# A masked-prefix-sum gather on one core: the rest rows move between the block places on TensorE, and the idle matmuls ahead of each wait are 10, 4 or none instead of 3

## The chip, the core and the metric

The kernel runs on one core of one Trainium2 chip. The metric is the device time of one execution in microseconds; lower is better. The kernel before took 84.66 us (median of four runs, 84.47 to 85.42).

## What is computed

```python
B, S, D = x.shape                       # 8, 8192, 512, float32
mask = (pos < lengths[:, None, None])   # rows past a sequence's length are zero
cs = np.cumsum(x * mask, axis=1)
midpoints = (lengths // 2).clip(0)
mid_features = cs[b_idx, midpoints, :]
return np.matmul(mid_features[:, None, :], w).squeeze(1)
```

Only row `lengths // 2` of each cumulative sum is used. So for each of the 8 sequences the kernel adds up its first `n = min(lengths // 2 + 1, lengths)` rows of 512 numbers, and multiplies the 8 sums by `w` (512 x 512). For the lengths of this case `n` is 570, 2690, 256, 2057, 905, 3772, 3859 and 571.

## The kernel before

**Blocks, places and rests.** Each sequence's `n` rows are cut into whole blocks of 512 rows (1 MB each; 128 partitions x 4 rows) and a rest of fewer than 512 rows. The sum over rows is a matmul: the weights are a 128 x 8 matrix that says to which of the 8 sequences a partition's rows belong, the rows are the moving operand, and `s_ps` in PSUM accumulates. A block takes four float32 matmuls (`add`, L490 to L494), which the profile shows as 8 matmul records, a pair of blocks as 16.

- The first block of sequences 0 and 1 is loaded blindly into `first`, before the lengths are known, and the last whole block of sequence 7 into `last`, in three pieces, at the very end.
- The other whole blocks (23 here) go in pairs through three *places* (`NS = 3`) of the buffer `xt`, 2 MB each. One round fills and uses the three places once, so 23 blocks take 4 rounds; the fourth has two full pairs and a single block in the third place.
- The rests go through two buffers of `rem` (`q = 0, 1`), two sequences a round, so 4 rounds as well. A rest is loaded by up to four smaller DMAs.

**Who does what.** SyncE (SP) loads the places: `load(k)` (L207 to L232) waits until place `k` is free, then issues its DMA, and after the rounds the three pieces of `last` (L246). ScalarE's queue loads the rests (L276, L288), each when its buffer is free. TensorE does the matmuls. VectorE (DVE) waits for a place's or a rest's matmuls, writes the next weights (`cur` L456, `cur_rem` L464) and by that frees the place or the rest's buffer. All the waits are on semaphores by hand; `take(eng, s, n)` (L144 to L146) waits for `n` and takes it off again. Each engine runs its own loop over rounds, in the order in which the code stands.

**TensorE's round** (L534 to L554) is: wait for rest 0 and add it, wait for rest 1 and add it; then for each place: three matmuls on constant data whose result nobody reads (`keep_busy`, L502 to L505, tile `idle_ps`, in bfloat16), the wait for the place (`take(pe, s_full[k], 32)`, L544), a branch on whether the place holds one block or two (L545), and the matmuls. `pairs` (L148 to L153) nests the places: a place that has no block any more ends the round.

**After the rounds** a one-element matmul (`tell`, L507 to L510) signals that the sum is complete. DVE copies `s_ps` to `s_sb` in two halves; TensorE transposes and folds it by matmuls (`fold_half`) and adds the pieces of `last` between them (`add_last`, L558), both into `t_ps`; DVE transposes into `t_sb`; TensorE multiplies by `w` into `o_ps`; DVE and ScalarE copy the two halves of the result to `o_sb`, and SP and ScalarE's queue store them.

## Time and profile before

| | |
|---|---|
| time, median of 4 runs | 84.66 us (84.47 to 85.42) |
| time of the profiled execution | 84.47 us |
| its span, first to last instruction | 82.5 us |
| PE busy / DVE busy / ACT busy | 56.1 / 15.2 / 5.5 us |
| matmuls of pairs (L492, `xt`) | 184 records, 25.1 us |
| idle matmuls (L505) | 48 records, 15.4 us |
| matmuls of rests (L492, `rem`) | 64 records, 9.9 us |
| moved by DMA | 31.26 MB |

The span is what the profiler sees of the execution; 1.97 us of the profiled time lie around it. A busy time is a sum over one engine, and the engines run beside each other, so busy times do not add up to the span. All positions below are microseconds from the start of the span. The notation `x16` after a group counts records, and `[3.52 <-PEq L146]` says that the engine sat idle for 3.52 us before it, released by the wait on line 146, which is that of `take`. `PEclk` is the share of TensorE's full clock that was granted.

### The profile page before, as it was taken

Reading aid. Unit: us, or ns where it says so; the run is one execution under the profiler, and the core shown is the slowest. Engines: PE = TensorE matmul, PEld = TensorE weight load, DVE = VectorE, ACT = ScalarE, POOL = GpSimd, SP = SyncE. Lnnn points to the kernel's source line nnn. Section 1 sums busy time; section 2 is a strip of 40 time slices with the busy share of each in tenths; the row PEclk is TensorE's granted clock in tenths of the full one; section 3 lists DMA queues with packets and bytes.
Section 4 is the critical chain, followed back from the end, with each engine's and each line's share of the span. In section 5 each row is a group of like instructions: output and inputs, shape, how many; then the busy total and the mean of one; then the engine's idle time right before and its main releaser. Section 6 shows DMA issues by size and latency. Waiting matters only on the chain. (4 is left out here: it accounts for less than half of the span.)

```text
span 82.5 us, 1486 instructions
## 1 busy us (share of the span) xinstructions
PE 56.1 (68%) x389; PEld 13.2 (16%) x389; DVE 15.2 (18%) x79; ACT 5.5 (7%) x6; POOL 1.6 (2%) x13
## 2 busy tenths in 40 slices
PE   2950699739990298930990799938408999799730
PEld 2300101002110121200110211111101112123510
DVE  2858888100000001000000001000000000001420
ACT  2991000000000000000000000000000000000020
POOL 5100000000000000000000000000000000000000
PEclk9999999999999999999759857999965569999996
DMA  2899999999999998999999999999999999899000
GB/s 36 306 413 437 461 419 415 443 439 397 445 437 405 397 476 361 433 417 437 441 401 436 442 413 421 453 425 397 456 405 446 397 437 453 373 403 366 1 0 16
DMA packets 3539, 31.26 MB, mean 379 GB/s; under 512 B 530, under 2 KB 546, under 8 KB 1202
## 3 DMA queue, kind: packets, MB, share of 16 engines
q1 hardware_dynamic: 2610, 27.27, 78.5%
q10 hardware_dynamic: 928, 3.97, 12.4%
q8 instruction: 1, 0.02, 0.1%
HBM read 31.23 MB, written 0.02 MB: 379 GB/s over the span
## 5 line engine op out<-in xcount | busy, mean ns | idle before, releaser
L492 PE MATMUL s_ps<-xt,cur 128*8 128x512 f32 x184 | 25.1, 666 | 15.3 <-PEq L146 15.3
L505 PE MATMUL idle_ps<-idle 128*128 128x512 bf16 x48 | 15.4, 436 | 3.6 <-DVE since L340 3.6
L492 PE MATMUL s_ps<-rem,cur_rem 128*8 128x512 f32 x64 | 9.9, 736 | 1.9 <-PEq L146 1.9
L456 DVE TENSOR_TENSOR cur<-since 128x16 f32 x9 | 1.7, 186 | 40.9 <-DVEq L146 40.9
L492 PEld LDWEIGHTS s_ps<-xt,cur 128*8 128x8 f32 x184 | 4.1, 91 | 28.9 <-issue 28.9
L505 PEld LDWEIGHTS idle_ps<-idle 128*128 128x128 bf16 x48 | 3.7, 104 | 21.1 <-issue 19.6
L310 ACT COPY o_sb<-o_ps 8x128 f32<-8x128 f32 x2 | 0.5, 258 | 72.6 <-PE o_ps L586 72.5
L261 ACT ACTIVATE rem<-rem 128x2048 uint32<-128x2048 uint32 x2 | 3.7, 1902 | 0.0
L492 PEld LDWEIGHTS s_ps<-rem,cur_rem 128*8 128x8 f32 x64 | 2.2, 113 | 9.6 <-issue 9.6
L516 PE MATMUL s_ps<-zero 1*128 1x512 f32 x2 | 2.1, 1136 | 1.6 <-DVE zero L340 1.6
L492 PE MATMUL s_ps<-first,cur_first 128*8 128x512 f32 x16 | 2.9, 816 | 0.0
L340 DVE COPY s_sb<-s_ps 128x256 f32<-128x256 f32 x2 | 0.8, 424 | 9.6 <-PE idle_ps L509 9.6
L464 DVE COPY cur_rem<-table 128x32 f32 x6 | 1.1, 181 | 8.1 <-DVEq L146 8.1
L498 PE MATMUL t_ps<-last,e_last 128*8 128x128 f32 x32 | 1.7, 273 | 0.0
L261 ACT ACT_TABLE_LOAD x1 | 1.3, 1283 | 1.4 <-PEq L607 1.4
L586 PE MATMUL o_ps<-wt,t_sb 128*8 128x128 f32 x32 | 1.1, 273 | 0.4 <-DVE t_sb L340 0.4
L340 DVE TENSOR_TENSOR part_a<-since,step_a 1x42 f32<-1x42 f32 (+1 forms) x2 | 1.1, 562 | 0.1
L498 PEld LDWEIGHTS t_ps<-last,e_last 128*8 128x8 f32 x32 | 0.9, 89 | 0.4 <-issue 0.3
L586 PEld LDWEIGHTS o_ps<-wt,t_sb 128*8 128x8 f32 x32 | 0.8, 89 | 0.7 <-issue 0.7
L498 PE MATMUL t_ps<-s_sb,fold 128*8 128x128 f32 x8 | 0.8, 274 | 0.1
L340 DVE TENSOR_TENSOR since<-item,begin 1x42 f32<-1x42 int32 (+1 forms) x2 | 0.8, 422 | 0.1
L519 PEld LDWEIGHTS n_ps<-len_f,ones 1*128 1x128 f32 x2 | 0.7, 333 | 1.0 <-DVE len_f L340 0.5
(66 smaller groups left out, 13.3 us busy)
## 6 DMA issues: line engine op xcount, KB each, us to landing
xt<-in_x_dram SPq DMA_DIRECT2D x10, 2048.0 KB, 12.7
xt<-in_x_dram SPq DMA_DIRECT2D x3, 1024.0 KB, 9.8
first<-in_x_dram SPq DMA_DIRECT2D x2, 1024.0 KB, 7.9
rem<-in_x_dram ACTq DMA_DIRECT2D x3, 512.0 KB, 8.6
wt<-in_w_dram ACTq DMA_DIRECT2D x1, 1024.0 KB, 4.8
rem<-in_x_dram ACTq DMA_DIRECT2D x3, 256.0 KB, 7.8
last<-in_x_dram SPq DMA_DIRECT2D x1, 512.0 KB, 6.1
last<-in_x_dram SPq DMA_DIRECT2D x2, 256.0 KB, 6.3
```

What stands on the lines that cost most here:

```text
L261: act.memzero(rem[:, q]).then_inc(s_rfree[q], 1)
L310: copy = act.copy(out=o_sb[1][:, j * P:(j + 1) * P], in_=o_ps[64 + 32 * j:64 + 32 * j + B, :P])
L340: do(*args, **kw).then_inc(s_dve, 1)
L456: dve.tensor_tensor(out=cur[:, k], in0=since[:, :B, here].rearrange("p b h -> p h b"), in1=since[:, 1:, here].rearrange("p b h -> p h b"), ...
L464: dve.tensor_copy(out=cur_rem[:, q], in_=rests[:, ds(dve.snap(of, min_val=1, max_val=B // 2 - 1), 1), q].rearrange("p o w -> p (o w)"),).t ...
L492: return pe.matmul(s_ps[32 * j:32 * j + B], lhsT=weights, rhs=rows, start=False, stop=False, skip_group_check=True, tile_position=(0, 32 * j))
L498: return pe.matmul(t_ps[32 * j:32 * j + B, :P], lhsT=weights, rhs=row[:, P * j:P * (j + 1)], start=False, stop=False, skip_group_check=Tru ...
L505: pe.matmul(idle_ps[:], lhsT=idle[:, :P], rhs=idle[:], start=True, stop=True)
L516: pe.matmul(s_ps[:], lhsT=zero[:], rhs=zero[:, :1].to_broadcast((1, D)), start=True, stop=False, skip_group_check=True)
L519: pe.matmul(n_ps[:, :B], lhsT=ones[:], rhs=len_f[:], start=True, stop=True).then_inc(s_pe, 1)
L586: mm = pe.matmul(o_ps[32 * j:32 * j + B, :P], lhsT=t_sb[:, kc, :B], rhs=wt[:, kc, j * P:(j + 1) * P], start=(kc == 0), stop=(kc == KC - 1) ...
```

## The change

TensorE's round now takes the places and the rests in turn: place 0, rest 0, place 1, rest 1, place 2. VectorE's loop follows in the same order, since it answers TensorE's signals one by one. The idle matmuls change from three ahead of each place to ten ahead of place 0, two ahead of rest 0, four ahead of place 1, and for place 2 four if it holds a pair and none if it holds a single block. Three idle matmuls ahead of the first round are dropped. The wait for a place now stands behind the branch on one block or two (once in each arm) where it stood ahead of it. `pairs` gets a parameter `most`, with which it does one place only; the places are no longer nested. The loads on SP and ScalarE's queue keep their code.

```diff
-    def pairs(eng, n, body, k=0):
-
-        if k < NS:
+    def pairs(eng, n, body, k=0, most=NS):
+
+        if k < most:
             with eng.If_cmp(n, 2 * k + 1, "IS_GE"):
                 body(k)
-                pairs(eng, n, body, k + 1)
+                pairs(eng, n, body, k + 1, most)
...
-            with dve.If_cmp(rest_rounds, 1, "IS_GE"):
-                for q in range(2):
-                    take(dve, s_rdone[q], 1)
-                    dve.tensor_copy(
-                        out=cur_rem[:, q],
...
-                    ).then_inc(s_rfree[q], 1)
-            pairs(dve, left, weights)
+            for k in range(NS):
+                pairs(dve, left, weights, k, k + 1)
+                if k < 2:
+                    with dve.If_cmp(rest_rounds, 1, "IS_GE"):
+                        take(dve, s_rdone[k], 1)
+                        dve.tensor_copy(
+                            out=cur_rem[:, k],
...
+                        ).then_inc(s_rfree[k], 1)
...
-        keep_busy()
+        BUSY = [10, 4, 0]
         pe.wait_ge(s_dve, DVE_MASK)
         with pe.Fori(0, rounds):
-            with pe.If_cmp(rest_rounds, 1, "IS_GE"):
-                for q in range(2):
-                    take(pe, s_rem[q], 16 * (len(PARTS) + 1))
-                    for j in range(G):
-                        mm = add(j, cur_rem[:, q, j * B:(j + 1) * B], rem[:, q, j])
-                    mm.then_inc(s_rdone[q], 1)
-
             def add_pair(k):
-                keep_busy()
-                take(pe, s_full[k], 32)
-                with pe.If_cmp(left, 2 * k + 2, "IS_GE"):
+                def second():
+                    take(pe, s_full[k], 32)
                     for j in range(G):
                         add(j, cur[:, k, 1], xt[:, k, 1, j])
+
+                keep_busy(BUSY[k])
+                with pe.If_cmp(left, 2 * k + 2, "IS_GE"):
+                    if k == NS - 1:
+                        keep_busy(4)
+                    second()
+                with pe.Else():
+                    take(pe, s_full[k], 32)
                 for j in range(G):
                     mm = add(j, cur[:, k, 0], xt[:, k, 0, j])
                 mm.then_inc(s_done[k], 1)
 
-            pairs(pe, left, add_pair)
+            for k in range(NS):
+                pairs(pe, left, add_pair, k, k + 1)
+                if k < 2:
+                    with pe.If_cmp(rest_rounds, 1, "IS_GE"):
+                        if k == 0:
+                            keep_busy(2)
+                        take(pe, s_rem[k], 16 * (len(PARTS) + 1))
+                        for j in range(G):
+                            mm = add(j, cur_rem[:, k, j * B:(j + 1) * B], rem[:, k, j])
+                        mm.then_inc(s_rdone[k], 1)
             less(pe, left, PER)
             less(pe, rest_rounds, 1)
```

## The prediction

> **What bounds the kernel now.** I read the slices of the page first, to see which resource is never idle.

> ```profile
> PE   2950699739990298930990799938408999799730
> PEclk9999999999999999999759857999965569999996
> DMA  2899999999999998999999999999999999899000
> ```

> PE has holes everywhere. The DMA row has none from the second slice to the 37th, where it stops for good. Four stretches (columns: length, busy time and count of each engine, granted clock, DMA share, GB/s) say how full it is:

> ```profile
> 10.00:76.00 66.00, 48.81 (x320) 10.02 (x323) 6.67 (x33) 0.00 (x0) 0.00 (x0) 0.90 1.01 423
> 20.00:22.00 2.00, 2.00 (x19) 0.43 (x11) 0.18 (x1) 0.00 (x0) 0.00 (x0) 1.00 1.04 442
> 22.00:24.00 2.00, 2.00 (x18) 0.34 (x16) 0.00 (x1) 0.00 (x0) 0.00 (x0) 1.00 1.01 426
> 66.00:68.00 2.00, 2.00 (x16) 0.33 (x8) 0.19 (x1) 0.00 (x0) 0.00 (x0) 0.63 0.98 418
> ```

> A share of 1.01 over 66 us: the 16 DMA engines have no gap that a better order on TensorE could fill. It is no lower around 22 and 67, where the longest idle places are being issued again (at 22.59 and 66.98). The chain of waits names PE for 7% of the span and begins only at 71.95, so I read the end one by one, in order of time (start, length, engine).

> ```profile
> 71.95 0.27 issue
> ...
> 72.22 1.90 PE L492 MATMUL s_ps<-xt,cur 128*8 128x512 f32 x16 [0.46 <-PEq L146]
> 74.06 0.82 PE L505 MATMUL idle_ps<-idle 128*128 128x512 bf16 x3
> 74.82 1.04 PE L492 MATMUL s_ps<-xt,cur 128*8 128x512 f32 x8
> 75.68 0.17 PE L509 MATMUL idle_ps<-idle 128*1 128x1 bf16 x1
> ...
> 76.97 0.26 PEld L498 LDWEIGHTS t_ps<-last,e_last 128*8 128x8 f32 x8
> ```

> and, from the answer on the tile `last`,

> ```profile
> L246 SPq DMA_DIRECT2D last<-in_x_dram x3: 332/333/333, 69.5 to 70.6; - x3
> DMA to landing us min/median/max: 6.1/6.2/6.4
> ```

> The third piece of `last` is issued at 70.57 and lands some 6.35 later, at 76.92. Its weights load starts at 76.97. So the end is set twice over: by the landing of the last bytes, and, with almost no slack, by the sum that `tell` reports at 75.68 (the two copies to `s_sb` take 0.88 from 75.97, and the second fold's weights load starts at 76.90).

> **The change part by part, in the last round, where it can count.** Landings are issue plus time to landing: place 2 of round 3 at 61.90 (49.39 + 12.5), round 4's places at 66.98 (54.78 + 12.2), 71.87 (59.07 + 12.8), 74.38 (66.98 + 7.4).
> - *Wait behind the branch.* From 71.95 the chain shows 0.27 of "issue": the branch that follows the wait. Now the branch is decided while the engine waits. Saved: 0 to 0.27; I take 0.22, since the load for `last`, a wait without a branch behind it, started 0.05 after its landing.
> - *Rest 1 between places 1 and 2.* 8 records, as in the single block: 75.68 - 74.82 = 0.86 added behind the last long wait. Before, this work lay ahead of it.
> - *No idle matmuls ahead of the single block.* 74.82 - 74.06 = 0.76 saved (0.25 each).
> - Sum for `tell`: -0.22 + 0.86 - 0.76 = -0.12, so 75.56. The single block landed at 74.38; TensorE reaches it at 71.87 + 0.14 + 1.84 + 0.86 = 74.7, so no new wait.
> - *For the end.* `add_last` of the third piece can't start before 76.92, and started at 76.97. Of the 0.12 at most 0.05 reaches the end. The profiled 84.47 becomes 84.42.

> This holds if TensorE is ready when place 1 lands. Walk from 61.90 at full clock, a pair at 72.22 to 74.06 = 1.84: pair to 63.9; ten idle matmuls, 2.5, to 66.4; place 0 landed 66.98, pair to 68.95; two idle 0.5, rest 0.86, four idle 1.0: 71.3. Slack 0.55 there and 0.6 at place 0. The eleven extra idle matmuls of a round (2.8) are thus paid from waits (3.52 ahead of 62.21 alone); without that cover they would cost all of it.

> *Earlier rounds.* Place 0 is worked on ahead of the rests, so it is free, and its next DMA issued, up to 2 earlier (two rests, 1.9 or more). SP's `last` pieces move ahead with it. The queue already holds 5 or more of transfers at each issue (22.59 against a next landing at 27.96; 66.98 against 71.87), so this shifts nothing at the end: taken at zero; if the queue did run dry now and then, it would be a gain.

> *Rests.* Their buffers are freed up to 3.5 later (rest 1 of round 3 at about 58.7 where the last ScalarE issue was at 56.0). They land within 5.6 to 9.4 of the issue: by 69 for rest 1, wanted at 73.9, and by 64 for rest 0, wanted at 69.4. Behind TensorE's wait for a rest now stand places 1 and 2, and behind those DVE's `cur` updates and SP's loads; with 5 of slack, nothing. DVE's operations (0.18 and 0.19 each) are the same ones in another order.

> *Branches.* A few more per round; they last 0.07 (not taken) to 0.24 and TensorE's queue is filled ahead of them: zero, bounded by 0.24.

> [...]

> **The clock.** I cut the span at the steps of the granted clock (third number from the end):

> ```profile
> 26.50:29.93 3.43, 1.66 (x16) 0.48 (x20) 0.00 (x0) 0.00 (x0) 0.00 (x0) 1.00 0.96 406
> 43.58:47.00 3.42, 1.20 (x12) 0.36 (x16) 0.00 (x0) 0.00 (x0) 0.00 (x0) 1.00 1.02 429
> 47.00:50.40 3.40, 3.40 (x20) 0.77 (x16) 0.32 (x2) 0.00 (x0) 0.00 (x0) 0.50 0.99 421
> 57.24:60.65 3.41, 1.45 (x11) 0.21 (x3) 0.19 (x1) 0.00 (x0) 0.00 (x0) 1.00 1.04 438
> 60.65:64.06 3.41, 1.85 (x12) 0.47 (x16) 0.00 (x0) 0.00 (x0) 0.00 (x0) 0.50 1.02 429
> 64.06:67.48 3.42, 3.42 (x24) 0.66 (x16) 0.19 (x1) 0.00 (x0) 0.00 (x0) 0.50 0.98 417
> ```

> A stretch of 3.41 with 1.45 busy or less is followed by half clock, one with 1.66 is not; from half clock a stretch with 1.85 busy doesn't lead back, a full one does. The change shortens the longest waits from 3.4-3.6 to 2.1-2.9 (place 2 of round 3: ready at 59.7, landed 61.9). Drops get rarer, not impossible. One stretch at half clock from 62.0 costs the pair and five idle matmuls about 1.6, and the slack of 0.6 + 0.55 takes most of it. So clock alone gives nothing to a kernel that waits for DMA.

> [...]

> **Rivals.**
> 1. *Slower: half clock for two stretches in round 4's approach.* Price, with the row of before (half clock 60.65 to 67.48, pair 62.21 to 65.58 = 3.37, idle at the same ratio 0.46 each): place 2's pair to 65.4; 4.5 idle to 67.5; 5.5 idle 1.35, pair 1.84, idle 0.5, rest 0.86, idle 1.0 to 73.0; pair, rest, block 3.56: `tell` at 76.55, 0.87 late and all of it on the end: 85.3, or 85.5 on the median. It decides once `tell` is later than about 75.7. For it: rest 1 and twice as many idle matmuls now stand in the way; against: the stretch after a drop would have to be half idle again, and behind 62.0 nothing is idle. 12%. Other delays of TensorE's last round, a fetch stall among them: 4%.
> 2. *Faster: earlier issues make the stream denser.* A stream 1.3% faster (428 for 423 GB/s over 66) ends 0.85 earlier: 83.8 on the median; at the 442 of the best row shown, 2.8 earlier. For it: single stretches exceed 423; against: the stretches around the latest issues aren't lower. 14%, small gains mostly.
> 3. *It does not change the waits:* clock falls as often, rests wait. Still 84.4 to 84.7, since DMA ends at 76.9.

> **How the numbers follow.** The profiled run lay 0.19 below the median of 84.66; forecast -0.05 to -0.12: 84.55 on the median, 84.2 to 85.0 by the spread of the runs. A measurement of this kernel tells about 1%, 0.85, from no change. Forecast and rival 3 within 1%: 70%. Slower 16%, faster 14%. The range takes in rival 1 and the edge of rival 2: 83.8 to 85.6.

> **What would show it.** After: DMA share still 1.0 to about 76.9; `tell` near 75.6, 16 + 8 + 8 records without an idle matmul ahead of it; the third `last` load right behind its landing. Wrong if DMA ends before 76.2, or if place 1 of round 4 lands while TensorE is still busy ahead of it.

## The result, and the profile after

The change made the kernel slower: 85.96 us (median of 12 runs, 85.39 to 86.61) against 84.64 us (17 runs), a ratio of 1.0147 with a 95% interval of 1.0111 to 1.0184. The forecast was 84.55 us in a range of 83.8 to 85.6. In all that follows the ratios and their intervals leave out a kernel's runs over 1.5% above its fastest; medians and lists of times hold every run.

The profiled execution took 85.49 us with a span of 83.7. Here are two rows of its slices and part of its DMA rows. The kernel before had one packet of the kind `instruction` (behind the stream, at 80.6) and 366 GB/s in the 37th slice:

```profile
DMA  2799999999999999999999999999999999995000
GB/s 35 294 407 423 470 419 454 411 423 407 462 392 423 442 421 370 427 454 431 423 423 442 395 446 399 411 442 423 427 427 431 414 455 395 411 389 211 4 8 8
DMA packets 3540, 31.28 MB, mean 374 GB/s; under 512 B 530, under 2 KB 546, under 8 KB 1202
...
q8 instruction: 2, 0.03, 0.2%
```

The stream is as dense as it was, up to 76. What is new is one packet more, of the kind `instruction`, and a tail behind the stream. The tail is seen best in stretches of half a microsecond (columns as in the prediction; the last two are DMA share and GB/s). Before:

```profile
76.00:76.50 0.50, 0.36 (x16) 0.07 (x11) 0.47 (x2) 0.00 (x0) 0.00 (x0) 1.00 0.46 164
76.50:77.00 0.50, 0.50 (x16) 0.35 (x20) 0.35 (x1) 0.00 (x0) 0.00 (x0) 1.00 0.00 0
```

and after:

```profile
76.00:76.50 0.50, 0.50 (x12) 0.10 (x3) 0.00 (x0) 0.00 (x0) 0.00 (x0) 1.00 0.80 291
76.50:77.00 0.50, 0.45 (x9) 0.01 (x1) 0.00 (x0) 0.00 (x0) 0.00 (x0) 1.00 0.08 29
77.00:77.50 0.50, 0.50 (x16) 0.33 (x16) 0.43 (x2) 0.00 (x0) 0.00 (x0) 1.00 0.06 25
77.50:78.00 0.50, 0.50 (x20) 0.33 (x16) 0.42 (x1) 0.00 (x0) 0.00 (x0) 1.00 0.03 12
```

A share of 0.06 is one sixteenth, and 25 GB/s are about one sixteenth of the 420 or so of the stream: for over a microsecond only as much moves as one of the 16 DMA engines carries, so I read that one engine still works and the other fifteen are done. The completion signals say since when. A load of this kernel signals 16 times, and TensorE's pair follows the last of them: in this profile place 1 of round 4 signals from 71.49 to 73.19, and its pair begins at 73.32. Before, the 16 signals of place 0 in round 4 come from 66.54 to 66.96; after, from 66.25 to 68.21. The first signals are not late, the last one is. In the first round the spread is still 0.5 to 0.8 us; from 32 on it is 1.6 to 2.7 in every load of SP's queue. In between lies the packet. The DMA part of the stretch from 31.3 to 32.5 (packets, MB, share of 16 engines):

```profile
q1 hardware_dynamic: 49, 0.38, 80.7%
q10 hardware_dynamic: 30, 0.03, 8.4%
q8 instruction: 1, 0.02, 5.6%
```

5.6% of 16 engines over 1.2 us are 1.07 us of one engine: 16 KB of instructions, fetched in the middle of the data at 31.34. And this is the end (order of time, TensorE):

```profile
71.90 1.04 PE L506 MATMUL idle_ps<-idle 128*128 128x512 bf16 x4
73.32 1.90 PE L493 MATMUL s_ps<-xt,cur 128*8 128x512 f32 x16 [0.39 <-PEq L146]
75.04 1.05 PE L493 MATMUL s_ps<-rem,cur_rem 128*8 128x512 f32 x8
75.89 1.05 PE L493 MATMUL s_ps<-xt,cur 128*8 128x512 f32 x8
76.75 0.17 PE L510 MATMUL idle_ps<-idle 128*1 128x1 bf16 x1
77.00 0.62 PE L499 MATMUL t_ps<-last,e_last 128*8 128x128 f32 x16
...
78.26 0.41 PE L499 MATMUL t_ps<-last,e_last 128*8 128x128 f32 x8
```

Pair, rest, block and `tell` follow one another as forecast (3.43 us, forecast 3.56 from the first matmul), but the pair begins at 73.32 where it was due at 72.0, because place 1 landed at 73.19 in place of 71.85. From the answer on the tile `last`:

```profile
L246 SPq DMA_DIRECT2D last<-in_x_dram x3: 333/333/333, 70.1 to 71.1; - x3
DMA to landing us min/median/max: 6.9/7.0/7.1
```

The third piece was issued at 71.1, half a microsecond later than before, and took 7.1 in place of 6.4: it landed at 78.21, 1.29 later, and the span is 1.2 longer.

The twelve times fall into two groups of six, 85.39 to 85.64 (granted clock 0.955 to 1.0) and 86.28 to 86.61 (0.928 to 0.939). The profile above is of the first.

### The profile page after: what moved, and what is told of

Same layout as the page of the kernel before. It is cut to its first block, busy times and chain, and to the rows that moved or that the text cites. A ratio compares the mean times of both kernels' runs of the same rounds, so it can differ in the third digit from the quotient of the medians.

```text
span 83.7 us, 1578 instructions
## 1 busy us (share of the span) xinstructions
PE 62.6 (75%) x426; PEld 16.1 (19%) x426; DVE 15.2 (18%) x79; ACT 5.5 (7%) x6; POOL 1.6 (2%) x13
## 5 line engine op out<-in xcount | busy, mean ns | idle before, releaser
L493 PE MATMUL s_ps<-xt,cur 128*8 128x512 f32 x184 | 24.3, 648 | 11.9 <-PEq L146 11.7
L506 PE MATMUL idle_ps<-idle 128*128 128x512 bf16 x85 | 23.8, 412 | 3.6 <-DVE since L340 3.6
L506 PEld LDWEIGHTS idle_ps<-idle 128*128 128x128 bf16 x85 | 7.1, 101 | 27.6 <-issue 22.1
L493 PE MATMUL s_ps<-rem,cur_rem 128*8 128x512 f32 x64 | 8.6, 607 | 0.0
L493 PE MATMUL s_ps<-first,cur_first 128*8 128x512 f32 x16 | 3.5, 975 | 0.0
L493 PEld LDWEIGHTS s_ps<-rem,cur_rem 128*8 128x8 f32 x64 | 1.4, 89 | 4.6 <-issue 4.6
L517 PEld LDWEIGHTS s_ps<-zero 1*128 1x128 f32 x2 | 0.5, 308 | 1.6 <-DVE zero L340 1.6
```

Of the source, the lines that this page charges most:

```text
L493: return pe.matmul(s_ps[32 * j:32 * j + B], lhsT=weights, rhs=rows, start=False, stop=False, skip_group_check=True, tile_position=(0, 32 * j))
L506: pe.matmul(idle_ps[:], lhsT=idle[:, :P], rhs=idle[:], start=True, stop=True)
L517: pe.matmul(s_ps[:], lhsT=zero[:], rhs=zero[:, :1].to_broadcast((1, D)), start=True, stop=False, skip_group_check=True)
```

## The experiments

Three theories are tested. Theory F (fetch): the loss is the instruction packet, which holds one DMA engine back for the rest of the stream; it comes because the longer program passes a certain length, which I took to be 512 instructions, an assumption that no run had shown. Theory S (schedule): it is the new order, whose rests and places are loaded at other times. Theory C (clock), for the second group: half clock in the last round. "Instructions" below are those of TensorE's program as built, 503 before and 537 after; the kernel's own end is 12 ahead of the total, since the program's closing instructions follow it.

**The changed kernel again** (no edit).

> The changed kernel once more, unchanged. Theory F (fetch): its profile shows a 16 KB instruction packet while the data stream runs, which before has only at 80.6 us after it; one of the 16 DMA engines falls behind by about that packet (1.07 us) and stays behind, so the 16 completions of a load are spread over 1.7 us in place of 0.4, and the last piece lands 1.3 us later. Expected: the packet again, 85.4 to 86.6. Of the twelve times six lie at 85.4 to 85.6 (granted clock 0.955 to 1.0) and six at 86.3 to 86.6 (0.93 to 0.94). Theory C (clock): the second 0.9 us is the half clock of rival 1 and a profile that falls there shows the signal of the complete sum about 0.9 us behind the landing chain. Theory S (schedule): the lateness comes from the order of rests and places; the packet is a bystander.

85.90 us (85.45 to 86.76, ratio 1.0142, interval 1.0079 to 1.0206), again three times at 85.5 and three at 86.3 to 86.8. The packet is there at 30.74, and the last piece lands at 78.26. The profile fell into the second group; it is read below, with the clock.

**Code that never runs**, in the kernel before.

```diff
         with pe.Else():
+            keep_busy(17)
             fold_half(0)
             fold_half(1).then_inc(s_pe, 1)
```

> The kernel before, with 17 idle matmuls (34 instructions) put into the arm of the last branch that these lengths never take: nothing more is executed, but TensorE's program has 537 instructions in place of 503, as many as the changed kernel. Theory F: an instruction packet turns up in the stream, the completions of later loads spread to 1.5 to 2 us, the time rises by 0.9 to 1.4 us, to 85.5 to 86.1. Theory S: nothing executed differs, so 84.6 to 84.7.

85.70 us (85.47 to 86.03), ratio 1.0129, interval 1.0088 to 1.0170. The arm is not executed (1486 instructions in the profile, as before), the order is that of before, and the price is there. Its DMA part, and a stretch of its tail:

```profile
q8 instruction: 2, 0.03, 0.2%
```

```profile
77.00:77.50 0.50, 0.50 (x15) 0.25 (x11) 0.00 (x0) 0.00 (x0) 0.00 (x0) 1.00 0.07 29
77.50:78.00 0.50, 0.50 (x21) 0.21 (x8) 0.34 (x1) 0.00 (x0) 0.00 (x0) 1.00 0.06 25
```

The packet came at 32.38; the signals of the last loads spread over 2.0 to 2.1 us; the last piece landed at 78.51. As nothing executed differs from the kernel before, theory S can't explain any of this.

**The changed kernel without the arm that is never taken.** Nothing that it executes differs.

```diff
-        with pe.Else():
-            fold_half(0)
-            fold_half(1).then_inc(s_pe, 1)
```

> The changed kernel with the arm that is never taken left out, and nothing else: every instruction that the changed kernel executes is executed here, in the same order, and TensorE's program is 18 instructions shorter (519; its last own instruction is number 507). Theory F with the boundary at 512: no instruction packet in the stream, spread of completions 0.4 to 0.6 us, and a median 1.0 to 1.3 us under the changed kernel's 85.9, at 84.5 to 85.0 (two groups 0.5 to 0.9 us apart stay, by theory C). If the order, the idle matmuls or the clock explain the whole of it: 85.9.

84.67 us (84.17 to 86.14), ratio 1.0000, interval 0.9963 to 1.0036. 18 instructions fewer, never executed in either, and 1.29 us are gone: the whole loss. The median stands between groups here too: six runs at 84.17 to 84.42, four at 84.93 to 85.08, and two later. Its DMA part has no row for instructions at all, and the end is the one that was forecast:

```profile
q1 hardware_dynamic: 2610, 27.27, 78.5%
q10 hardware_dynamic: 928, 3.97, 12.2%
```

```profile
72.06 1.90 PE L493 MATMUL s_ps<-xt,cur 128*8 128x512 f32 x16 [0.59 <-PEq L146]
73.77 1.05 PE L493 MATMUL s_ps<-rem,cur_rem 128*8 128x512 f32 x8
74.63 1.05 PE L493 MATMUL s_ps<-xt,cur 128*8 128x512 f32 x8
75.49 0.17 PE L510 MATMUL idle_ps<-idle 128*1 128x1 bf16 x1
...
77.03 0.41 PE L499 MATMUL t_ps<-last,e_last 128*8 128x128 f32 x8
```

`tell` at 75.49 (forecast 75.56); the third piece lands at 76.98, and its matmuls start at 77.03.

**Where the boundary is.** The never-executed lines again, 4, 12 and 22 instructions in place of 34 (`keep_busy(2)`, `(6)`, `(11)`).

> The kernel before with 4 instructions (2 idle matmuls) in the arm that is never taken: TensorE's program has 507 instructions. [...] If every added instruction costs, or the code behind the loop being moved at all, 84.6 to 85.7.

> The same with 12 instructions (6 idle matmuls): 515 instructions, just past 512. Theory F: the whole price at once, a packet in the stream, spread of completions 1.5 to 2 us, 85.4 to 86.0, as with 34 instructions. A cost by the amount of code: a third of the 1.2 us, 84.9.

> The kernel before with 22 instructions (11 idle matmuls) in the arm that is never taken: 525 in all, the last own instruction number 513. With 12 it was 515 and 503, and nothing happened. Boundary at 512 for the program's own end: the packet and 85.4 to 86.0. If the boundary lies elsewhere (between 525 and 537 in all): 84.5.

| instructions (own end) | packet in the stream | third piece lands | median us | ratio, interval |
|---|---|---|---|---|
| 503 (491), before | none | 76.92 | 84.64 | |
| 507 (495) | none | 76.97 | 84.55 | 0.9982, 0.9945 to 1.0019 |
| 515 (503) | none | 76.96 | 84.63 | 1.0004, 0.9968 to 1.0040 |
| 525 (513) | at 44.10 | 78.32 | 85.96 | 1.0148, 1.0100 to 1.0197 |
| 537 (525) | at 32.38 | 78.51 | 85.70 | 1.0129, 1.0088 to 1.0170 |

It is a step, not a slope. My expectation for 515 was wrong in what it counted: the total passes 512 there and nothing happens. The step lies where the kernel's own end passes from 503 to 513; the changed kernel without the arm, with its own end at 507, has no packet either. The 512 that I had assumed lies between 507 and 513. But the own end was taken as the measure only after 515 had shown no packet, and the count holds branch labels too, so a boundary at 512 was not shown; the step is.

**One engine held back by hand.** To the kernel before, one or two 16 KB loads into one partition of an unused buffer are added, which are one packet each, in ScalarE's loop, in the second round; with `range(2)`, and a wait for 32, for two. The buffers and a semaphore are declared beside them.

```diff
+            with act.If_cmp(pair, 4, "IS_EQ"):
+                for i in range(1):
+                    act.dma_start(out=extra[i][:], in_=xf[8 * i:8 * i + 8].rearrange("(o r) d -> o (r d)", o=1)).then_inc(s_extra, 16)
...
+            act.wait_ge(s_extra, 16)
```

> The kernel before, with one more load in ScalarE's queue in the second round of rests: 16 KB of x into one partition of a buffer that nobody reads. It is one packet, so one DMA engine carries it, as with the instruction packet; no instruction packet in the stream. Theory F says that it is the load on one engine that counts, whoever sends it: a 16 KB packet takes 0.62 us in the median in the trace of before, so 0.6 us later (to 1.1, what the instruction packets took), 85.1 to 85.6, with the completions of later loads spread to 1.0 to 1.5 us. If all engines share it: 16 KB of 31.26 MB, 0.04 us, 84.55.

> The same with two such loads of 16 KB, on the same engine: twice the lag, 1.2 us (to 2.2), 85.7 to 86.7. If all engines share them: 84.6.

84.94 us (ratio 1.0033, interval 1.0010 to 1.0057) and 85.59 us (1.0102, 1.0066 to 1.0138); no instruction packet in the stream in either. The packets took 0.65 us in the one run and 0.66 and 0.61 in the other; the third piece landed at 77.54 and 78.12, 0.6 and 1.2 later than before. The tail of the second one, again at one sixteenth:

```profile
76.50:77.00 0.50, 0.50 (x13) 0.16 (x9) 0.00 (x0) 0.00 (x0) 0.00 (x0) 1.00 0.07 25
77.00:77.50 0.50, 0.50 (x21) 0.24 (x12) 0.31 (x1) 0.00 (x0) 0.00 (x0) 1.00 0.06 25
```

16 KB among 31.26 MB cost 0.6 us at the landing when one engine carries them, and twice as many twice that. The first median fell short of what I expected (84.94 for 85.1 to 85.6, and 0.34 above the 84.60 of the kernel before beside it), the second just short of 85.7; the landings are of one execution each, and why the first median rose by less than its landing was not found. So the lag does not need instructions: packets of data of the same size, each carried by one engine as I read the tail, bring it as well. The same bytes spread over all 16 engines were not tried; that one engine is behind rests on the share of one sixteenth and on the doubling.

**The short changed kernel, and the order alone.** The first is the changed kernel without the arm and without the nine idle matmuls ahead of the loop (502 instructions). The second has the changed order, but three idle matmuls ahead of each place and none ahead of a rest, without the arm (497). The second, beside the arm:

```diff
-        BUSY = [10, 4, 0]
+        BUSY = [3, 3, 3]
...
-                    if k == NS - 1:
-                        keep_busy(4)
...
-                        if k == 0:
-                            keep_busy(2)
```

> The changed kernel with its TensorE program cut to 502 instructions: the arm for sequences without a last block, which these lengths never take, is left out (its part of the computation is for other lengths), and so are the nine idle matmuls ahead of the loop. Round order and the idle matmuls of the rounds stay as changed. Theory F: no instruction packet in the stream, spread of completions 0.4 to 0.6 us, 84.4 to 84.7; half the runs may still be 0.9 us later by theory C. Theory S: still 85.4 to 86.6.

> Order alone: rests between the places and the wait behind the branch as changed, but three idle matmuls ahead of each place as before and none ahead of a rest; the arm that is never taken is left out (497 instructions). Theory F: no packet, 84.4 to 84.8, or up to 0.9 us more where the three idle matmuls ahead of the single block and rest 1 add up (0.76 + 0.86 - 0.76 + ... : the complete sum is due at 76.3 in place of 75.7, so up to 85.3). Theory S: if the order is at fault 85.4 or more, if the idle matmuls are, 84.6.

84.97 us (ratio 1.0031, interval 0.9998 to 1.0064) and 85.27 us (1.0089, 1.0055 to 1.0124; 85.03 to 87.21, three of the twelve above 86.5); no packet in either. The order alone does cost: rest 1 and the three idle matmuls now both stand behind place 1's pair, `tell` is at 76.44 (76.3 expected). In the change, leaving out the idle matmuls ahead of the single block makes up for that: `tell` came at 75.49 above. The short kernel shows the two groups bare, five runs at 84.48 to 84.53, six at 84.97 to 85.08 and one at 85.62, and its profile is of the later one: `tell` at 76.33.

**The second group.** The granted clock of that profile, cut at its steps:

```profile
61.42:64.83 3.41, 3.41 (x22) 1.01 (x14) 0.19 (x1) 0.00 (x0) 0.00 (x0) 1.00 1.00 420
64.83:68.24 3.41, 1.39 (x13) 0.38 (x16) 0.00 (x0) 0.00 (x0) 0.00 (x0) 1.00 1.01 422
68.24:71.66 3.42, 3.42 (x18) 0.25 (x10) 0.00 (x0) 0.00 (x0) 0.00 (x0) 0.50 0.97 413
```

The wait ahead of place 0 of round 4 was 2.02 us, 1.39 of the stretch were busy, and half clock followed just when the last round's work was due. By the granted clock, the other late runs of this group are alike (0.947 to 0.951, the early five 0.967 to 1.0). The changed kernel's second profile shows the same: 1.41 busy from 65.90 to 69.31, half clock to 72.73, `tell` at 77.65, 0.90 behind the first profile's. Three runs test it. The first, in the short changed kernel:

```diff
-        BUSY = [10, 4, 0]
+        BUSY = [15, 0, 0]
...
-                        if k == 0:
-                            keep_busy(2)
```

> The short changed kernel (arm that is never taken and idle matmuls ahead of the loop left out, 500 instructions) with its idle matmuls put elsewhere: fifteen ahead of place 0, none ahead of rest 0 and place 1; place 2 as changed. Theory C: the later half of the runs of the short changed kernel (84.97 to 85.08 beside 84.5) comes from the wait ahead of place 0 of round 4, 2.02 us there after ten idle matmuls, which lets the clock fall while the last round's work is still ahead; with five more the wait is 0.9 us, and behind it 1.5 us less work stands ahead of place 1. Expected: all runs at 84.4 to 84.6, no second group, the signal of the complete sum at 75.5 to 75.8. If the second group has another cause, the median stays at 84.97.

84.59 us, but in two groups: seven at 84.26 to 84.68 (by these the ratio is 0.9977, interval 0.9951 to 1.0002) and five at 85.86 to 86.10 (clock 0.914 to 0.934). A miss. The wait ahead of place 0 is gone in its profile, but without the idle matmuls ahead of place 1 there is one of 2.21 us there, still later. That the late runs come from a drop in this wait was not shown, since the profile is of an early run.

The second, in the changed kernel without the arm:

```diff
-        BUSY = [10, 4, 0]
+        BUSY = [0, 4, 0]
```

> The changed kernel without the arm that is never taken, and with no idle matmuls ahead of place 0 (the other idle matmuls as changed; 499 instructions, no packet expected). Theory C: without the ten, the wait ahead of place 0 of the last round grows from 1.5-2.0 to some 3.8-4.3 us, so that a stretch of 3.41 us with under 1.5 busy lies in it in every run, and half clock is granted when the last round's work begins or during it. Expected: hardly a run at 84.2 to 84.4 (six of twelve there with the ten), most at 84.9 or above, the granted clock under 0.95; where the drop comes early enough in the wait to be lifted by 69, 84.4. If the second group has nothing to do with that wait, half of the runs stay at 84.2 to 84.4.

86.07 us, all runs at 85.64 to 87.01 (ratio 1.0159, interval 1.0104 to 1.0214). None is left in the early group. The profile:

```profile
61.86:65.27 3.41, 0.62 (x8) 0.00 (x0) 0.19 (x1) 0.00 (x0) 0.00 (x0) 1.00 0.97 408
65.27:68.68 3.41, 1.54 (x8) 0.32 (x12) 0.00 (x0) 0.00 (x0) 0.00 (x0) 0.50 1.00 419
68.68:72.09 3.41, 3.41 (x18) 0.42 (x14) 0.00 (x0) 0.00 (x0) 0.00 (x0) 0.50 1.02 429
```

The wait ahead of place 0 is 4.66 us, half clock is granted for two stretches, `tell` comes at 77.22 although the last piece lands at 77.06, as early as in the good runs. This profile is of the slowest of the six, 87.01 us, of which 2.95 lie outside its span of 84.06, against 1.97 before; that extra microsecond is not the clock's. The spans of the six are 83.7 to 84.4, those of the kernel before beside it 82.5 to 83.5.

The third, in the short changed kernel:

```diff
-        BUSY = [10, 4, 0]
+        BUSY = [15, 4, 0]
```

> The short changed kernel (arm that is never taken and idle matmuls ahead of the loop left out) with fifteen idle matmuls ahead of place 0 in place of ten, the two ahead of rest 0 and four ahead of place 1 kept; 512 instructions in all, its own end at 500. Theory C: the wait ahead of place 0 shrinks to 0.5-0.9 us and the one ahead of place 1 stays at 0.6, so no stretch of 3.41 us with under 1.5 busy is left in the last round: the group at 84.95 to 85.1 goes, 84.2 to 84.6 in at least ten of twelve runs, a median 0.2 under the kernel before. A drop in the wait ahead of place 2 of round 3 can still make TensorE late: it has 1.1 to 1.5 us of slack for about 1.6 us lost, so a few runs at 84.6 to 85.0. If the second group has another cause, half the runs at 84.95 or above.

84.41 us (84.24 to 85.38), ratio 0.9991, interval 0.9962 to 1.0021. Seven runs at 84.24 to 84.44, three to 84.73, two above; I had expected ten up to 84.6. The group at 85 is gone but for these two, and the clock lies at 0.97 to 1.0 in all twelve. In its profile:

```profile
65.27:68.68 3.41, 3.02 (x23) 0.85 (x21) 0.00 (x0) 0.00 (x0) 0.00 (x0) 1.00 1.00 420
```

Ten idle matmuls fewer bring the group to every run, five more nearly end it. This bears out theory C for the wait ahead of place 0; the late runs of the first of these three tests, and the two above 84.8 here (clock 0.972 and 0.973), have no profile and stay open.

**The two good pieces, in the order of before**, without the arm: the wait behind the branch, and no idle matmuls ahead of a single block in place 2.

```diff
-                keep_busy()
-                take(pe, s_full[k], 32)
+                if k < NS - 1:
+                    keep_busy()
                 with pe.If_cmp(left, 2 * k + 2, "IS_GE"):
+                    if k == NS - 1:
+                        keep_busy()
+                    take(pe, s_full[k], 32)
...
+                with pe.Else():
+                    take(pe, s_full[k], 32)
```

> The order of before, with two pieces of the change alone: the wait for a place behind the branch, and no idle matmuls ahead of a single block in place 2; the arm that is never taken is left out, 494 instructions. By my sum the complete sum is signalled 0.2 to 0.3 us earlier (single block at 74.38 + 0.14, or behind place 1's pair), at 75.4, and the end, which waits for the last piece, gains 0.05: 84.4 to 84.6 against 84.5. If the end depends on the sum alone, 84.2 to 84.3. Fewer runs above 84.8 than before has (6 of 23), since the tail has 0.3 us of slack.

84.43 us (84.32 to 84.97), ratio 0.9979, interval 0.9951 to 1.0007. `tell` at 75.53; one run of 12 above 84.8, where the kernel before had 14 of 35 beside it. This and the short kernel with fifteen are the best medians seen, 0.14 and 0.15 under before in their own comparisons. Neither interval excludes 1, so neither is shown to be faster.

## Why the prediction was wrong, point by point

- **The failed step** is the one on the longer program. The forecast gives the longer program no price beyond its branches, "zero, bounded by 0.24", and names "a fetch stall" only among the delays of TensorE, at 4% together. No run shows such a stall. In the profile above the branch at the loop's end lasts 0.239 us at most, 0.241 before; the longest branch inside the loop, 0.338 at 27.40, falls into the matmuls of a pair (27.35 to 29.25). What the runs showed in its place is a price on the resource that bounds the kernel. One 16 KB packet, 1.07 us long, on one of 16 engines as I read the tail, delays the later loads of SP's queue, since each is complete only with the last of its 16 signals, now 1.6 to 2.7 us behind the first: against the same kernel without the arm, the three pieces of `last` land 1.2 to 1.3 us later (78.21 for 76.98 the third). The DMA share stays near 1 up to 76, so there is no gap in which the engine could catch up. The bound was taken from the wrong engine.
- The signs that the prediction named for being wrong, a faster stream or a late TensorE, do not show this loss: in the profile above the DMA ended later, not before 76.2, and TensorE still waited for place 1 of round 4, for 0.39 us. Only in the second group TensorE was late: in the repeated run's profile place 1 landed at 73.23, and its pair began at 74.22.
- **The price of the longer program**, in this kernel, whose DMA has no gap, was 1.2 to 1.4 us by the medians (85.70 and 85.96 with 34 and 22 instructions more, beside 84.51 and 84.60; 85.96 for the changed kernel, beside 84.67 without the arm). The runs place the step between an own end at 507 and at 513; why it is there they do not show.
- **"so this shifts nothing at the end: taken at zero"**, of the earlier place loads, failed too, at a smaller size. The end of the stream stayed, but its inside moved: in the short kernel place 2 of round 3 lands at 60.66 in place of 61.90, while place 0 of round 4 stays at 66.85. The wait between them, 0.6 in my walk, is 1.5 to 2.0; ten idle matmuls also took 2.3 us there in place of 2.5. The granted clock is lower in about half of the runs, and without the packet these are 0.5 to 0.7 us later.
- **Rival 1** had the place, the last round at half clock, and the size: 0.87 for `tell` by its sum, 0.90 between the changed kernel's two profiles. It named the wrong wait (ahead of place 2 of round 3 in place of the next one), gave it two stretches where one is enough, and 12% where half of the runs have it. It adds to the packet's loss and does not explain it.
- **What was right**: that DMA sets the end; that `tell` gains a little (0.19 for 0.12 forecast, 75.49 for 75.68, where neither packet nor clock interferes) and that almost none of it reaches the end; 0.14 from landing to first matmul behind the reordered wait (71.92 to 72.06); that the extra idle matmuls cost nothing while they fit into waits. Without the arm, the changed kernel's program is short enough, and its ratio to before is 1.0000.
- **Smaller slips**, which do not change the forecast: in rival 2, 428 GB/s for 423 is 1.2%, 0.8 us over 66, not 1.3% and 0.85; the stretch at 66 to 68 is lower than the mean (0.98 and 418); from 66.98 to the landing at 71.87 are 4.9 us, not 5.
- **The clock's limit**, 1.45 us of work in a stretch of 3.41 us, is not sharp. Of the stretches at full clock between 10 and 80 us in the profiles of the two kernels, cut as above, those with 0.82 to 1.20 us were followed by half clock and those with 1.63 or more were not. In between both happened: in the profile of the changed kernel 1.43 us from 48.87 to 52.28 had no such effect, and 1.43 us from 59.10 to 62.52 had, as had the prediction's 1.45 and the 1.39 and 1.41 of the second group, with waits of 2.0 us in them.

## What to carry to other kernels

When DMA has no gap, ask of every edit what else it sends through the DMA engines, and on how many of them: here one packet of 1.07 us, on one engine as I read it, delayed the loads of SP's queue, which signal in 16 parts, to the end (the last landing 1.29 us later). Code that is never executed was not free here once it took the program past a certain length (22 instructions in the kernel before cost 1.4 us by the medians, 12 nothing), so look at the length before and after, and read the row of instruction packets and the spread of a load's completions. The idle matmuls that paid in these runs were those ahead of the last round's wait for place 0, where a fall of the clock would have met the last round's work (84.67 us with the ten, 86.07 without them).
